# Neighbourhood attention with the weights of its second and last pairs traced ahead, two late query tiles turned in score banks, and two low parts on VectorE

## The chip, the cores and the metric

The kernel runs on one core of a Trainium2 chip. Its time is the device time in microseconds of one execution, and the median of several runs is compared. TensorE multiplies and transposes, VectorE and ScalarE work on what it leaves in its PSUM banks, GpSimd works on SBUF alone, and SyncE (SP) issues most of the transfers between HBM and SBUF.

## What is computed

Two layers of a hybrid backbone act on 1024 latent tokens (a grid of 16 rows and 64 columns) and 128 context tokens, 1152 in all, 1024 features wide, in float32. The first layer has four mLSTM heads and eight grouped-query attention heads, the second sixteen neighbourhood attention heads. Cut to what matters here:

```python
# layer 0, grouped-query part: dense softmax attention of each query block over latent and cached keys
s = einsum('bkgqd,bksd->bkgqs', qi, k) * scale
o = einsum('bkgqs,bksd->bkgqd', softmax(s), v)
# layer 1: each latent token attends to an 8 x 16 window of the grid, with a bias by offset, and to all context keys
q, k, v, z = split(h @ w_in_c, 4)
p = softmax(concat([s_loc + bias, s_ctx]))
o = p_loc @ v_win + p_ctx @ vc
y = (o * silu(z)) @ w_out
# both layers: x = x + gate * rmsnorm(y)
```

## The kernel before, in words

Every projection keeps float32 precision by splitting: an operand is cast to a high part, and the low part is the difference. A product is then three matmuls (high by high, low by high, high by low). `feat` (L367 to L369) gives a projection with features on partitions, 24 matmuls of 128x384 for each of three token chunks; `tok` (L382 to L384, through `rows_by`) gives it with tokens on partitions, 24 matmuls a token tile. `weights` (L121) loads one 512 KB block into one of two `raw` buffers over SP's queue (L126), casts the high part on ScalarE (L115) and subtracts for the low part (L116), on GpSimd unless `vec` is `"lo"`, then on VectorE. The raw buffer is free for the next load when the low part is done.

SBUF tiles of up to 1152 values a partition come from a shared pool of 35 slots (`u`, tag "u"). The three chunks of the normalised input h hold 18 of them in the second layer until the last projection is done. PSUM has eight banks: two for projections (`pj`), three for scores (`s`), one each for `tr` and `ptr`, in which transposes are turned, and one for outputs (`o`).

The program is written as a trace. A scheduler orders each engine's instructions anew, with what was traced earlier ahead of what was traced later, as operands, slots and banks come free in its own simulation; so what is traced behind can still fill a wait of what is traced ahead. On TensorE the grouped-query attention alone is under a manual schedule: its order is the order of the trace.

**Grouped-query attention** (`gqa`, L962). Nine query tiles for each of two groups are projected and turned in `gqa_q`; `turned` (L871) transposes a tile in two halves into bank `tr` or `ptr`, by the tile's parity, casts its high part on ScalarE (L878) and subtracts on VectorE (L879). Tiles 7 and 8 of the second group are kept back in a list and turned in the first iteration of `gqa`. An iteration takes two query tiles: it computes the scores of the next two (L915), turns the probabilities of its own two in ten steps of up to four transposes each (`gqa_turn`, over the banks `tr`, `pj`, `ptr`, `pj` in a cycle, evacuated by ScalarE at L946, each fifth by VectorE at L944), and multiplies them by the values (`gqa_apply`, L955). In the third and fourth head block each iteration also takes one step of `ahead` (L1417), which loads, casts and splits the eight blocks of the first layer's `w_out`.

**First output projection** ("out0", L1422). `load_y` brings a token tile of the mixer's output through a `raw` buffer (L1064), casts it on ScalarE and subtracts on VectorE; `out_half` multiplies it by `w_out` (L382 to L384, operands `yh`, `yl`). One raw buffer holds the gate row (`load_gg`, L1103) for most of that phase.

**Neighbourhood attention** ("na", L1456). The heads go in eight pairs. `na_proj` (L1112) projects a pair's values, queries and keys and `na_pair` (L1224) attends: for each of eight column blocks `na_unit` computes scores of two heads (L1267), adds the bias (VectorE, L1273), takes the exponential (ScalarE, L1275) and its scale (VectorE, L1276; GpSimd, L1277), turns it in `tr` and `ptr` (L107) and multiplies by the values (L1290); a context unit follows (L1031, L1050). The biases of a pair, one for each head, are loaded at the start of `na_pair` (L1230). Pairs 1, 3 and 5 project the values of two pairs at once with `tok` from two blocks of `w_v` (L1184), pair 7 its own with `feat`. A pair's weights are traced inside its own `na_proj`, behind the attention of the pair before; W(0) is the query block, W(1) the keys', W(2) the values', W(3) the gate's.

Of the kernel before, what the change touches and what calls it, by code (L numbers as in the profile page):

```python
# [19 lines left out]
D = 1024  # L20
# [19 lines left out]
class Kern:  # L40
# [378 lines left out]
    def gates(self, gT):  # L419
# [40 lines left out]
        nc.vector.tensor_tensor_scan(b, cst, lf, 0.0, ALU.mult, ALU.add)  # L460
        A, WK, F, M, W = (q5[:, j, :] for j in range(5))
        nc.vector.tensor_tensor(A, li, b, ALU.subtract)
# [43 lines left out]
        nc.vector.tensor_scalar(mi[:72, 1:2], M[:, P - 1 : P], -1.0, None, ALU.mult)  # L506
        nc.scalar.activation(W, M, AF.Exp, bias=mi[:72, 0:1], scale=-1.0)
        nc.scalar.activation(WK, A, AF.Exp, bias=mi[:72, 1:2])
# [342 lines left out]
    def gqa_q(self, h, g, w, Qs, early):  # L851

        nc = self.nc
        ahead = None
        rhs = lambda k: tuple(x[:, (k % 4) * 256 : (k % 4 + 1) * 256] for x in w[k // 4])
        Q = []
        for i in range(NT):
            if i == NT - 4:
                ahead = self.gqa_weights(2) if g == 0 else self.gqa_gate(0)
            if i in (1, 3, 5) and g:  # L860
                n = len(early)
                q0 = Qs[0][n // 2][:, n % 2]
                early.append([])
                for _ in self.gqa_scores([q0[:, hh] for hh in range(2)], 0, lambda s: self.u(s, n="pr"), early[-1]):
                    pass
            ps = self.tok(h, i, rhs, 256)
            q = self.norm_rope(ps, 4, 0, i)
            if i % 2 == 0:
                Q.append(self.u([P, 2, 4, P], F32R, n="Q"))

            def turned(i=i, q=q, Qt=Q[-1]):  # L871
                pt = self.ps(("tr", "ptr")[i % 2])[:, :256]
                for j in range(2):
                    self.flipped(pt[:, j * P : (j + 1) * P], q[:, 2 * j : 2 * j + 2].rearrange("p a b -> p (a b)"))
                for hh in range(2):
                    x = pt[hh * DHB : (hh + 1) * DHB].rearrange("p (a b) -> p a b", b=P)
                    hi, lo = (Qt[r * DHB : (r + 1) * DHB, i % 2, hh::2, :] for r in (g, 1 - g))
                    nc.scalar.copy(hi, x)  # L878
                    nc.vector.tensor_tensor(lo, x, hi.bitcast(F32), ALU.subtract)  # L879

            if g and i in (7, 8):
                self.turned.append(turned)
            else:
                turned()
        return Q, ahead
# [76 lines left out]
    def gqa(self, Q, gz, early, between):  # L962

        kv = lambda j: j // 2
        V = lambda t, j: t[..., kv(j) * DHB : (kv(j) + 1) * DHB]
        q = lambda j, i: [Q[kv(j)][i // 2][:, i % 2, 2 * (j % 2) + hh, :] for hh in range(2)]
        place = (lambda s: self.t("pr", 4, s)), (lambda s: self.u(s, n="pr"))
        todo = iter([(j, i) for j in range(4) for i in range(8)])  # L970

        def tiles(out):
            for j, i in itertools.islice(todo, 2):
                if early:
                    out.append(early.pop(0))
                else:
                    prs = []
                    yield from self.gqa_scores(q(j, i), kv(j), place[i % 2], prs)
                    out.append(prs)

        prs, banks = [], ("tr", "pj", "ptr", "pj")
        for _ in tiles(prs):
            pass
        for j in range(4):
            y = self.ytile()
            for i in range(0, 8, 2):
                if i % 4 == 0:
                    po = self.ps("o")
                nxt, pts = [], ([], [])
                steps = tiles(nxt)  # L990
                turns = self.gqa_turn(prs, pts, banks)
                if i == 4:
                    ctx = self.ctx_steps([self.gqa_terms(x, kv(j), [self.KstP[:, b] for b in range(4)]) for x in q(j, 8)], [V(self.VP, j)] * 2, self.pt, banks=("s", "s"))
                next(steps, None)
                next(steps, None)
                for n, _ in enumerate(turns):
                    if (j, i, n) in ((0, 0, 5), (0, 0, 7)):
                        self.turned.pop(0)()
                    if i == 4 and n == 7 or i == 6 and n == 5:
                        next(ctx)  # L1000
                    if (i, n) != (4, 7):
                        next(steps, None)
                for _ in steps:
                    pass
                self.gqa_apply(pts, V(self.V, j), po[:, i % 4 * P : (i % 4 + 2) * P])
                if i == 6:
                    cpo = next(ctx)
                prs = nxt
                if j >= 2:
                    next(between, None)  # L1010
                if i % 4:
                    self.put_y(4 + j, slice((i - 2) * P, (i + 2) * P), po, gz, y)
            self.put_y(4 + j, slice(8 * P, NT * P), cpo, gz, y)
            gz = self.gqa_gate(j + 1) if j < 3 else None
        return y
# [58 lines left out]

    def w_out(self, l, j):

        return self.weights(self.a["w_out"][l, j], ("", "lo")[j % 2] if l else "")

    def out_half(self, y, w, n, o, ss, gg):
        nc = self.nc  # L1080
# [26 lines left out]
    def na_weights(self, p, b, raw=None):  # L1107
        if raw is not None:
            self.nc.sync.dma_start(raw, self.a["w_c"][4 * p + b])
        return self.weights(self.a["w_c"][4 * p + b], raw=raw)  # L1110

    def na_proj(self, h, p, w):  # L1112
        nc, a = self.nc, self.a
        W = lambda b: self.na_weights(p, b)
        two = lambda t: t[2 * p : 2 * p + 2].rearrange("h t d -> t h d")
        v2 = lambda t: t.rearrange("p (h d) -> p h d", d=DHB)

# [6 lines left out]
        if 0 < p < 7 and p % 2 == 0:  # L1124
            self.feat(h, W(3), zev)
        v = self.u([P, NT, P], n="v") if p in (0, 7) or p % 2 else self.v2
# [12 lines left out]
        q = [self.u([P, T], F32R, n="q") for _ in range(2)]  # L1139
# [40 lines left out]
        if p == 7:  # L1180
            self.feat(h, W(2), vev)
        elif p % 2:

            w = [self.weights(a["w_v"][p // 2, :, q * D : (q + 1) * D]) for q in range(2)]  # L1184
            for i in range(NT):
                ps = self.tok(h, i, lambda k: tuple(x[:, (k % 4) * 256 : (k % 4 + 1) * 256] for x in w[k // 4]), 256)
                nc.scalar.copy(v[:, i, :], ps[:, :P])
                nc.vector.tensor_copy(self.v2[:, i, :], ps[:, P:])
        elif p == 0:

            for cs in ((0, 1), (2,)):
                self.feat(h, w[0], zev, cs)
                self.feat(h, w[1], vev, cs)
        nc.sync.dma_start(two(a["out_nv"]), v2(v[:, 8, :]))
        late = []
        if p < 7:
            self.feat(h, W(0), qev)
            w = W(1)
            self.key_stack2(v2(kc), kx)
            self.feat(h, w, kev)  # L1200
            if p % 2:
                wz = W(3)
                late = [lambda c=c: self.feat(h, wz, zev, [c]) for c in range(NC)]
        else:

            wq, wz = W(0), W(3)
            for w, e, cs in ((wq, qev, [0]), (wz, zev, [0, 1]), (wq, qev, [1])):
                self.feat(h, w, e, cs)
            w = W(1)
            self.key_stack2(v2(kc), kx)  # L1210
            self.feat(h, w, kev)

            late = [lambda w=w, e=e, c=c: self.feat(h, w, e, [c]) for w, e, c in [(wq, qev, 2), (wz, zev, 2)]]

        def terms(hh, j, k0, n):

            x = q[hh][:, j * P : (j + 1) * P]

            ks = lambda t: t[:, k0 : k0 + 4].rearrange("p (a b) k -> p b a k", a=2) if k0 in (2, 6) else t[:, k0 : k0 + n]
            return (x, ks(k[hh])), (x, ks(k[2 + hh]))  # L1220
# [419 lines left out]
```

## Time and profile before

| what | value |
|---|---|
| median of 3 runs | 1527.03 us (1527.02 to 1527.52) |
| profiled execution | 1527.66 us, its span 1525.9 us |
| TensorE busy | 1489.1 us, 98% |
| VectorE, ScalarE, GpSimd busy | 54%, 47%, 29% |
| mean granted TensorE clock | 0.999 |

The profile is of one execution. A row of the timeline gives start and length in us, engine, line, operation, what is written and read, and how often; in brackets the engine's idle time before it and what ended that. PEld is TensorE's loading of weights, which runs beside its matmuls. The end of a matmul is modelled. A row of groups gives, behind the bar, the busy time in us, the mean of one instruction in ns, and the engine's idle time before them.

### The profile page before, as it was taken

The numbers are of one execution on the slowest core, as the hardware profiler recorded it, in microseconds if no ns is written. First come the engines' busy times: TensorE is split into PE (matmuls) and PEld (weight loads), VectorE is DVE, ScalarE is ACT, GpSimd is POOL, SyncE is SP. The second block draws the span as 40 slices with busy tenths as digits, with TensorE's granted clock in tenths as the row PEclk, the third lists the DMA queues.
The fourth block names the chain that finished last, engine by engine and source line by source line (L and its number), as shares of the span: only waits on it lengthen the run. The fifth ranks groups of instructions, "written<-read, shape, count | busy, mean of one in ns | idle before, by whom it ended". The sixth has DMA issues, their size and how long they took to land.

```text
span 1525.9 us, 27070 instructions
## 1 busy us (share of the span) xinstructions
PE 1489.1 (98%) x10139; PEld 1370.8 (90%) x10139; DVE 828.0 (54%) x2387; ACT 711.9 (47%) x1767; POOL 449.3 (29%) x644
## 2 busy tenths in 40 slices
PE   7899999999999999999999999999999999999998
PEld 5799999999999888887888989999999999988786
DVE  5833887963457766665565352535344434445532
ACT  4533535263445777786454352534344344345411
POOL 0001202011135655675224141323132222233200
PEclk9999999999999999999999999999999999999999
DMA  9203546332311000122423222131213121125342
GB/s 378 79 15 130 190 147 239 137 122 75 111 48 44 1 32 24 44 67 70 151 98 137 74 62 80 42 98 31 85 38 104 33 82 69 54 90 167 106 131 83
DMA packets 73284, 143.80 MB, mean 94 GB/s; under 512 B 15737, under 2 KB 44609, under 8 KB 73153
## 3 DMA queue, kind: packets, MB, share of 16 engines
q1 hardware_dynamic: 68566, 126.91, 25.0%
q10 hardware_dynamic: 4586, 15.16, 2.7%
q8 instruction: 80, 1.31, 0.3%
q14 instruction: 52, 0.42, 0.1%
HBM read 115.47 MB, written 21.86 MB: 90 GB/s over the span
## 4 chain that ended last, share of the span: by engine, by line
PE 49%; DMA 1%; DVE 1%; ACT 1%; POOL 1%; issue 0%; DVEq 0%; POOLq 0%; ACTq 0%
PE pj L367 7%; PE pj L368 7%; PE pj L369 7%; PE pj L383 6%; PE pj L382 6%; PE pj L384 6%; PE o L1290 4%; PE s L1267 3%; PE ptr L107 2%; PE tr L107 2%; DMA y<-yd 1%; POOL wlo L116 1%; DMA raw<-in_w_out_dram 0%; DVE sb L1273 0%; POOL pr L925 0%
## 5 line engine op out<-in xcount | busy, mean ns | idle before, releaser
L367 PE MATMUL pj<-hh,whi 128*128 128x384 f32 x1168 | 400.2, 343 | 1.8 <-ACT qT L102 1.2
L368 PE MATMUL pj<-hl,whi 128*128 128x384 f32 x1168 | 397.0, 340 | 0.0
L369 PE MATMUL pj<-hh,wlo 128*128 128x384 f32 x1168 | 395.8, 339 | 0.5 <-DVE wlo L116 0.4
L367 PEld LDWEIGHTS pj<-hh,whi 128*128 128x128 f32 x1168 | 219.6, 188 | 5.5 <-ACT qT L102 1.8
L369 PEld LDWEIGHTS pj<-hh,wlo 128*128 128x128 f32 x1168 | 219.4, 188 | 1.9 <-DVE wlo L116 0.9
L368 PEld LDWEIGHTS pj<-hl,whi 128*128 128x128 f32 x1168 | 219.6, 188 | 1.2
L1277 POOL TENSOR_SCALAR sb<-sb,sm 128x512 f32<-128x512 f32 (+1 forms) x128 | 85.1, 671 | 247.7 <-DVE sm L1276 238.7
L116 POOL TENSOR_TENSOR wlo<-raw,whi 128x1024 fp32r<-128x1024 f32 x43 | 103.0, 2400 | 132.8 <-ACT whi L115 113.7
L925 POOL TENSOR_SCALAR pr<-pr,smg 128x384 f32<-128x384 f32 x192 | 110.0, 591 | 73.9 <-PE pj L107 41.0
L382 PE MATMUL pj<-whi,hh 128*128 128x256 f32 x432 | 122.5, 284 | 0.3 <-DVE nr L783 0.3
L383 PE MATMUL pj<-wlo,hh 128*128 128x256 f32 x432 | 122.5, 284 | 0.0
L384 PE MATMUL pj<-whi,hl 128*128 128x256 f32 x432 | 122.2, 283 | 0.0
L382 PE MATMUL pj<-whi,yh 128*128 128x512 f32 x288 | 114.3, 397 | 2.9 <-DVE o L1085 1.5
L916 DVE CUSTOM_DVE_ANT_0 pr<-s,zero 128x384 f32<-128x384 f32 x192 | 103.8, 553 | 24.3 <-PE s L915 20.9
L383 PE MATMUL pj<-wlo,yh 128*128 128x512 f32 x288 | 113.9, 395 | 0.0
L1275 ACT ACTIVATE sb<-sb,sm 128x512 f32<-128x512 f32 (+1 forms) x128 | 88.9, 695 | 52.9 <-DVE sm L1273 49.3
L384 PE MATMUL pj<-whi,yl 128*128 128x512 f32 x288 | 113.3, 394 | 0.0
L915 PE MATMUL s<-Kst,Q 128*128 128x384 f32 x384 | 107.8, 372 | 1.1 <-ACT pt L1035 1.1
L254 DVE CUSTOM_DVE_ANT_0 mj<-wm,cb 128x512 f32<-128x512 f32 x128 | 89.5, 699 | 5.2 <-DMA wm<-in_w_modT_dram 3.0
L115 ACT CAST whi<-raw 128x1024 fp32r<-128x1024 f32 x77 | 79.7, 1046 | 19.5 <-DMA raw<-in_w_v_dram 6.6
L1273 DVE CUSTOM_DVE_ANT_1 sb<-s,bias 128x512 f32<-128x512 f32 (+1 forms) x112 | 72.9, 664 | 24.9 <-PE ptr L107 12.1
L382 PEld LDWEIGHTS pj<-whi,hh 128*128 128x128 f32 x432 | 81.3, 188 | 1.4 <-issue 0.5
(350 smaller groups left out, 2901.3 us busy)
## 6 DMA issues: line engine op xcount, KB each, us to landing
wm<-in_w_modT_dram SPq DMA_DIRECT2D x32, 512.0 KB, 5.2
raw<-in_w_c_dram SPq DMA_DIRECT2D x25, 512.0 KB, 3.5
raw<-in_w_ab_dram SPq DMA_DIRECT2D x20, 512.0 KB, 3.5
e<-rbd ACTq DMA_DIRECT2D x12, 768.0 KB, 7.7
bias<-in_na_bias_dram SPq DMA_DIRECT2D x16, 576.0 KB, 4.1
wm<-in_w_mod_dram SPq DMA_DIRECT2D x16, 512.0 KB, 9.8
raw<-in_w_out_dram SPq DMA_DIRECT2D x16, 512.0 KB, 3.6
y<-yd SPq DMA_DIRECT2D x18, 448.0 KB, 3.4
```

The costliest lines, as they stand in the source:

```text
L116: (eng_lo or nc.gpsimd).tensor_tensor(lo, src, hi.bitcast(F32), ALU.subtract)
L254: nc.vector.tensor_tensor_reduce(junk, w[:, b, :], cb[:, r, :], 1.0, 0.0, ALU.mult, ALU.add, mp[:, hf, q // 4, 2 * (q % 4) + b, r : r + 1])
L367: nc.tensor.matmul(ps[:, :CW], a, hh, start=k == 0, stop=False)
L368: nc.tensor.matmul(ps[:, :CW], a, hl, start=False, stop=False)
L369: nc.tensor.matmul(ps[:, :CW], b, hh, start=False, stop=k == KB - 1)
L382: nc.tensor.matmul(ps[:, :width], hh, a, start=k == 0, stop=False)
L383: nc.tensor.matmul(ps[:, :width], hh, b, start=False, stop=False)
L384: nc.tensor.matmul(ps[:, :width], hl, a, start=False, stop=k == KB - 1)
L915: nc.tensor.matmul(s[:, :CW], x, y, start=part == 0, stop=part == 1)
L916: nc.vector.tensor_tensor_reduce(pr[:, c, :], s[:, :CW], zero, -1.0, -NEG, ALU.add, ALU.min, m3[:, c : c + 1])
L925: nc.gpsimd.tensor_scalar(pr[:, c, :], pr[:, c, :], r, 0.5, ALU.mult, ALU.mult)
L1275: nc.scalar.activation(x, x, AF.Exp, bias=nm, scale=-1.0, accum_out=r)
```

## The change

Four edits, of which the first two go together:

- the two kept-back query tiles are turned in a score bank (`s`) and no longer in `tr` and `ptr`, and called behind the eighth and tenth turn of the first iteration instead of the sixth and eighth;
- in the first layer the blocks 6 and 7 of `w_out` get their low part on VectorE; the second layer's blocks alternate as before;
- the two value blocks of pair 1 are traced at the end of pair 0's projections, ahead of pair 0's attention;
- the value, query and gate blocks of pair 7 are traced at the end of pair 6's projections, ahead of pair 6's attention; its key block stays where it was.

```diff
--- before.py
+++ after.py
@@ -869,7 +869,7 @@
                 Q.append(self.u([P, 2, 4, P], F32R, n="Q"))
 
             def turned(i=i, q=q, Qt=Q[-1]):
-                pt = self.ps(("tr", "ptr")[i % 2])[:, :256]
+                pt = self.ps("s" if g and i in (7, 8) else ("tr", "ptr")[i % 2])[:, :256]
                 for j in range(2):
                     self.flipped(pt[:, j * P : (j + 1) * P], q[:, 2 * j : 2 * j + 2].rearrange("p a b -> p (a b)"))
                 for hh in range(2):
@@ -994,7 +994,7 @@
                 next(steps, None)
                 next(steps, None)
                 for n, _ in enumerate(turns):
-                    if (j, i, n) in ((0, 0, 5), (0, 0, 7)):
+                    if (j, i, n) in ((0, 0, 7), (0, 0, 9)):
                         self.turned.pop(0)()
                     if i == 4 and n == 7 or i == 6 and n == 5:
                         next(ctx)
@@ -1074,7 +1074,7 @@
 
     def w_out(self, l, j):
 
-        return self.weights(self.a["w_out"][l, j], ("", "lo")[j % 2] if l else "")
+        return self.weights(self.a["w_out"][l, j], "lo" if (j % 2 if l else j >= 6) else "")
 
     def out_half(self, y, w, n, o, ss, gg):
         nc = self.nc
@@ -1109,9 +1109,12 @@
             self.nc.sync.dma_start(raw, self.a["w_c"][4 * p + b])
         return self.weights(self.a["w_c"][4 * p + b], raw=raw)
 
+    def v_weights(self, p):
+        return [self.weights(self.a["w_v"][p // 2, :, q * D : (q + 1) * D]) for q in range(2)]
+
     def na_proj(self, h, p, w):
         nc, a = self.nc, self.a
-        W = lambda b: self.na_weights(p, b)
+        W = lambda b: self.w7[b] if p == 7 and b in self.w7 else self.na_weights(p, b)
         two = lambda t: t[2 * p : 2 * p + 2].rearrange("h t d -> t h d")
         v2 = lambda t: t.rearrange("p (h d) -> p h d", d=DHB)
 
@@ -1181,7 +1184,7 @@
             self.feat(h, W(2), vev)
         elif p % 2:
 
-            w = [self.weights(a["w_v"][p // 2, :, q * D : (q + 1) * D]) for q in range(2)]
+            w = self.wv if p == 1 else self.v_weights(p)
             for i in range(NT):
                 ps = self.tok(h, i, lambda k: tuple(x[:, (k % 4) * 256 : (k % 4 + 1) * 256] for x in w[k // 4]), 256)
                 nc.scalar.copy(v[:, i, :], ps[:, :P])
@@ -1211,6 +1214,11 @@
             self.feat(h, w, kev)
 
             late = [lambda w=w, e=e, c=c: self.feat(h, w, e, [c]) for w, e, c in [(wq, qev, 2), (wz, zev, 2)]]
+
+        if p == 0:
+            self.wv = self.v_weights(1)
+        if p == 6:
+            self.w7 = {b: self.na_weights(7, b) for b in (2, 0, 3)}
 
         def terms(hh, j, k0, n):
```

## Rows read from the trace of the kernel before

**Rows 1.** The page, part 1: busy us (share of the span) and instructions.

```profile
PE 1489.1 (98%) x10139; PEld 1370.8 (90%) x10139; DVE 828.0 (54%) x2387; ACT 711.9 (47%) x1767; POOL 449.3 (29%) x644
```

**Rows 2.** Sums by window; header names the columns, (x) counts instructions.

```profile
core 0: us, PE busy (x) PEld busy (x) DVE busy (x) ACT busy (x) POOL busy (x), PEclk, DMA share, GB/s
512.70:523.60 10.90, 7.42 (x55) 6.01 (x54) 7.54 (x30) 10.46 (x27) 9.13 (x16) 1.00 0.00 0
702.20:714.60 12.40, 12.40 (x113) 9.26 (x114) 6.04 (x14) 8.44 (x17) 8.65 (x9) 1.00 0.39 121
714.60:716.30 1.70, 0.37 (x7) 0.13 (x3) 0.91 (x3) 0.94 (x1) 0.00 (x0) 1.00 0.05 13
859.90:877.30 17.40, 17.40 (x102) 17.40 (x101) 6.19 (x13) 5.50 (x12) 1.50 (x2) 1.00 0.26 86
877.30:888.00 10.70, 8.09 (x43) 5.44 (x41) 9.36 (x30) 8.50 (x20) 5.61 (x7) 1.00 0.15 34
888.00:919.60 31.60, 31.60 (x323) 30.40 (x323) 12.11 (x40) 13.15 (x35) 12.50 (x14) 1.00 0.20 64
1337.10:1355.60 18.50, 16.79 (x189) 14.28 (x188) 11.13 (x35) 11.33 (x27) 7.05 (x10) 1.00 0.06 22
```

**Rows 3.** Timeline, TensorE, first iteration of grouped-query attention.

```profile
519.71 0.41 PE L107 MATMUL ptr<-cc,nr 128*128 128x128 f32 x2 [0.95 <-ACT pt L946]
519.95 0.60 PE L107 MATMUL pj<-cc,pr 128*128 128x128 f32 x4
520.39 0.60 PE L107 MATMUL tr<-cc,pr 128*128 128x128 f32 x4
522.44 0.41 PE L107 MATMUL tr<-cc,nr 128*128 128x128 f32 x2 [1.45 <-ACT pt L946]
...
523.57 4.11 PE L955 MATMUL o<-pt,V 128*64 128x256 f32 x36
```

**Rows 4.** Timeline, ScalarE, the same stretch.

```profile
519.43 1.29 ACT L922 ACTIVATE pr<-pr,smg 128x1152 f32<-128x1152 f32 x1
...
523.32 0.59 ACT L946 COPY pt<-pj 128x512 f32<-128x512 f32 x1
```

**Rows 5.** Timeline, four engines, up to the first output projection.

```profile
705.37 1.06 ACT L115 CAST whi<-raw 128x1024 fp32r<-128x1024 f32 x1
...
709.45 2.37 POOL L116 TENSOR_TENSOR wlo<-raw,whi 128x1024 fp32r<-128x1024 f32 x1
...
711.85 11.51 SPq L1064 DMA_DIRECT2D y<-yd  x3
...
715.31 0.94 ACT L115 CAST yh<-y 128x896 fp32r<-128x896 f32 x1 [4.08 <-DMA y<-yd]
...
716.30 0.50 PE L382 MATMUL pj<-whi,yh 128*128 128x512 f32 x1 [1.33 <-ACT yh L115]
```

**Rows 6.** Groups by line and shape, whole span.

```profile
L367 PE MATMUL pj<-hh,whi 128*128 128x384 f32 x1168 | 400.2, 343 | 1.8 <-ACT qT L102 1.2 <-DVE kl L1170 0.3 <-DVE vT L104 0.2
...
L116 DVE TENSOR_TENSOR wlo<-raw,whi 128x1024 fp32r<-128x1024 f32 x34 | 42.6, 1254 | 12.9 <-ACT whi L115 9.6 <-DMA wm<-in_w_mod_dram 2.3 <-PE pj L368 0.8
```

**Rows 7.** Timeline, four engines, attention of pair 0.

```profile
880.36 0.47 PE L1267 MATMUL s<-k,q 128*128 128x512 f32 x1 [0.99 <-DVE sm L1276]
...
887.98 0.48 PE L1267 MATMUL s<-k,q 128*128 128x512 f32 x1 [0.97 <-issue]
...
860.84 0.33 SPq L126 DMA_DIRECT2D raw<-in_w_v_dram  x1
...
887.03 1.03 ACT L115 CAST whi<-raw 128x1024 fp32r<-128x1024 f32 x1
...
889.16 2.40 POOL L116 TENSOR_TENSOR wlo<-raw,whi 128x1024 fp32r<-128x1024 f32 x1
```

**Rows 8.** Timeline, two engines, attention of pair 6.

```profile
1303.15 0.33 SPq L126 DMA_DIRECT2D raw<-in_w_c_dram  x1
...
1352.77 1.99 ACT L115 CAST whi<-raw 128x1024 fp32r<-128x1024 f32 x2
```

## The prediction

> **What bounds the kernel.** I read the page's busy line first: TensorE is busy 98% of the span and no other engine over 54% [rows 1]. So only time in which TensorE starts no matmul can be won, and I looked for that stretch by stretch: the list of TensorE's waits gives their names, the sums by window their size, the timeline what ends each. Before 512 us the diff changes nothing. After it the windows show four stretches with TensorE idle [rows 2]: 512.7 to 523.6 (7.42 us busy of 10.90), 714.6 to 716.3 (0.37 of 1.70), 877.3 to 888.0 (8.09 of 10.70) and 1337.1 to 1355.6 (16.79 of 18.50). The stretch right behind the third, 888.0 to 919.6, is the same kind of work and full. In each of the four the diff changes something; I call them A, B, C and D.
>
> A visible gap is shorter than the loss, since a matmul's modelled end runs past the start of the next: four transposes stand with 0.60 us, yet the next four start 0.44 us after them [rows 3]. So I add 0.16 us to each gap.
>
> **A, the two late query tiles.** Tiles 7 and 8 of the second query group are turned by two transposes each, placed by hand between the ten turns of the first iteration. Tile 7's wait 0.95 us and tile 8's 1.45 us [rows 3]; both wait for ScalarE's copy out of the very bank that they are to write, which a turn filled just before. ScalarE is the late one: busy 10.46 of the stretch's 10.90 us [rows 2], with an exponential of 1.29 us ahead of the copies [rows 4]. The change gives both a score bank (no more scores are due in this iteration, so these banks are empty) and calls them two turns later. Removed: 0.95 + 1.45 + 2 x 0.16 = 2.7 us. Added: nothing; transposes, casts and subtractions are as many as before. What is late next: the value matmuls (L955) behind the turns need ScalarE's last copy, which ended at 523.91, and they started at 523.57 [rows 3, 4]. ScalarE may keep that time, with the tiles' short casts ahead of the copy. But in their 4.11 us the value matmuls come to that copy only after some two thirds, 2.7 us, so they can begin near 521.2 even then: 2.4 us won. The score banks must be empty when the next scores come, behind the value matmuls, and ScalarE and VectorE have those 4.11 us for it. Bounds: 0 (if the copies slip with the casts) and 2.7; I take 2.7, since the copies' rows lie close.
>
> **B, two low parts on VectorE.** At the first output projection TensorE idles 1.33 us until ScalarE has cast y, which waited 4.08 us for y's load; that load was issued at 711.85, when GpSimd's subtraction for the last w_out block (709.45, 2.37 us) had freed the raw buffer [rows 5]. On VectorE the same subtraction takes 1.25 us [rows 6], and its input, the cast of 705.37, is there at 706.43. VectorE is busy 6.04 of 12.40 us there [rows 2], so two subtractions, 2.5 us, fit; even if the second waits 1.25 us for other work it ends by 709.0, and the load starts 2.8 us earlier. Load and cast take 716.30 - 711.85 = 4.45 us and TensorE could start at 714.8 (the gap taken off), so 710.3 is early enough. Removed 1.33 + 0.16 = 1.5 us. GpSimd is relieved of 2 x 2.37 us where it feeds the last turns. Bounds 0 (the load is late for another reason) and 1.5; I take 1.5.
>
> **C, value weights of pair 1 ahead.** In 877.3 to 888.0 pair 0's attention runs almost alone: 2.61 us idle in five gaps, the first at 880.36, the last at 887.98, between score matmuls that wait for the softmax chain on the other engines [rows 2, 7]. What covers attention later, pair 1's value projection, needs both weight halves. The second half's raw load was issued at 860.84, yet its cast ran at 887.03 and its low part ended at 891.56 [rows 7]; it is traced behind attention. Traced ahead, the cast can follow the load, near 865 to 870, and two casts and two low parts (2 x 1.03 and 2 x 2.40 us) leave the softmax chain too. Where they go, 859.9 to 877.3, ScalarE is busy 5.50 and GpSimd 1.50 of 17.40 us [rows 2], under the key projection, which TensorE computes without a gap. On SP's queue pair 0's biases may come behind the raw load of 860.84; a load of about this size lands in 3.5 us (711.85 to 715.31, [rows 5]), so 869 at the latest, ahead of the scores. Shared slots: 18 for h, 4 for pair 0's gate, values and queries, 4 for its two weights, 4 new ones, 2 biases: 32 of 35. Removed: 2.61 + 5 x 0.16 = 3.4 us. Bounds 0 and 3.4; I take 3.4, because the next stretch, where the same filler is at hand, has no gap at all. The filler lasts: behind 919.6 the value projection still goes on alone, so using 3.4 us of it early uncovers nothing.
>
> **D, weights of pair 7 ahead.** The same in pair 6's attention: its filler, pair 7's value projection, is spent at 1337.1. Behind it 1.71 us are idle in four gaps, while the raw loads of the next weights, the last issued at 1303.15, wait for casts at 1352.77 [rows 2, 8]. Cast ahead they give 72 matmuls of 0.34 us less 0.16 [rows 6], 13 us of filler, for gaps of 1.71 + 4 x 0.16 = 2.35 us. One gap of the four stands among transposes of the value tiles, which weights don't touch; I take three quarters, 1.8 us, with bounds 0 and 2.35. GpSimd gets up to three low parts (7.2 us) ahead of pair 6's scalings, again under the key projection.
>
> **Sum.** 2.7 + 1.5 + 3.4 + 1.8 = 9.4 us. The profiled execution took 1527.66 us (span 1525.9), so 1518.3; the median of the runs is 0.63 us lower: **1517.6 us**. TensorE's granted clock is 1.00 in every window, the upper of its two levels (2.4 GHz).
>
> **Rivals.**
> First: the scheduler keeps the casts behind the exponentials, or lays the fillers elsewhere. For it: raw loads stood issued for 26 us in C and 49 us in D before their casts [rows 7, 8], so something other than the load decides. Then A and B alone: 2.7 + 1.5 = 4.2, 1522.8 us; with half of C and D 1520.2.
>
> Second, slower: the slots run out. Pair 6's six new weight tiles are traced ahead of its two biases: 18 for h, 4 for the score rings, 4 for the pair, 4 for its own weights and these 6 are 36 of 35. The biases then wait for the key projection's weights, the fillers are spent while attention waits, and it runs uncovered at the pace of 877.3 to 888.0, 3.4 us lost in 10.70. Over as long an attention as pair 0's, 877.3 to 919.6, that is 13.4 us, 11.0 more than D's 2.35 now. With A, B and C won (7.6) it comes to 1530.5. It decides as soon as the biases land after the fillers end. Against: SP may still issue the biases first, since they wait for nothing but slots, and pair 0 has room for all.
>
> Third: as much is lost in new places, since the last pair has gaps behind VectorE and ScalarE that any reordering moves. Then 1524 to 1530, no change.
>
> Fourth: more is won. In the four stretches weight loads are busy far less than matmuls: 10.90 - 6.01, 1.70 - 0.13, 10.70 - 5.44 and 18.50 - 14.28, 15.9 us free together, of which a covered stretch would keep 3.8% (31.60 - 30.40) [rows 2]. If all that were won, 14.4 us: 1512.6. Against: between the gaps matmuls already follow at full pace. The Trainium skill (Perfetto Trace Analysis, Identifying the Most-Contended Engine) speaks for it: matmul busy share is called a poor measure of headroom there, the busy share of weight loads a good one; by it the sum is 14.4 where mine is 9.4.
>
> **How the numbers follow.** My forecast, all four stretches mostly won, 60%: 1515.5 to 1520. First rival 19%, 1520 to 1524. Fourth 7%. Third 9%. Second 5%. A measurement here can tell about 0.2%, 3.05 us, from no change; so faster is the forecast, the first and the fourth: 86%, same 9%, slower 5%. The range goes from a little under the forecast's own to most of the first rival: 1514.5 to 1523.5.
>
> **What would show it.** A: the transposes of tiles 7 and 8 without idle time before them, L955 starting near 521 instead of 523.57. B: the y load issued before 710 and no gap before L382. C: both casts of the value weights before 877, and L382 to L384 between pair 0's score matmuls from the first one on. D: the casts of pair 7 before 1320, and L367 to L369 between 1337 and 1352. Wrong would be: biases landing after the key projection, TensorE waiting for a low part, or gaps of the same sum elsewhere.

## The result and the profile after

The changed kernel takes 1517.74 us (median of 6 runs, 1515.79 to 1520.05), the kernel before 1527.16 us beside it (6 runs, 1526.24 to 1529.14); the ratio is 0.9937 with an interval of 0.9924 to 0.9950. The forecast was 1517.6 us. The profiled execution took 1517.94 us, its span 1516.2.

The page, part 1, of the changed kernel, against [rows 1]:

```profile
PE 1486.5 (98%) x10139; PEld 1371.4 (90%) x10139; DVE 827.4 (55%) x2389; ACT 712.6 (47%) x1767; POOL 447.1 (29%) x642
```

Sums by window of the changed kernel, against [rows 2]; the stretches are moved to where the same work now stands (A, the start of B, C, D and the end of D):

```profile
core 0: us, PE busy (x) PEld busy (x) DVE busy (x) ACT busy (x) POOL busy (x), PEclk, DMA share, GB/s
511.30:519.40 8.10, 7.04 (x54) 6.03 (x52) 6.30 (x27) 7.98 (x22) 7.43 (x13) 1.00 0.01 2
709.50:711.90 2.40, 2.40 (x18) 1.39 (x17) 0.82 (x4) 0.00 (x0) 0.00 (x0) 1.00 0.36 99
872.00:882.60 10.60, 10.60 (x79) 9.94 (x79) 6.57 (x24) 5.95 (x15) 3.42 (x6) 1.00 0.14 32
...
1328.60:1347.00 18.40, 18.40 (x155) 17.44 (x155) 8.34 (x27) 8.33 (x19) 4.47 (x7) 1.00 0.03 12
1347.00:1356.00 9.00, 8.21 (x99) 7.25 (x95) 5.28 (x13) 4.92 (x11) 1.98 (x3) 1.00 0.26 89
```

B, C and D are full now; in A 1.06 us stay idle (two waits that stood before the turns and that nothing touches), and 0.79 us at the end of D: 0.44 us ahead of transposes of probabilities and 0.35 us ahead of transposes of values, both behind ScalarE's copy at L102.

Idle time alone does not say what a part is worth. Every trace here has 10139 TensorE matmul records, so the record with the same number (counted from 0) marks the same amount of work done; each stretch of the table also holds the same matmuls before and after, but for the bank of the two query tiles. The table gives the time from start to start of such records, in us (the first column from the start of the span), for the two kernels and all experiments; the letters are the parts of the change that fall into a stretch:

```
record      0-3250   -3500  -4750  -5000   -5500   -6250   -8750   -9500  -10138
                       A              B               C               D
before        504.55  36.08 162.27  45.92  100.23  105.31  333.67  109.96  121.25
before_again  504.47  36.07 162.27  46.15  100.24  106.31  333.67  110.02  121.41
after         503.18  33.29 162.27  45.19  100.33  101.57  334.02  108.17  121.52
after_again   503.59  33.30 162.28  45.63  100.33  101.57  334.02  107.93  120.68
a_only        503.14  33.31 162.29  45.99  100.34  105.53  333.63  110.33  120.74
a_bank        505.87  33.64 162.27  45.92  100.23  105.35  333.67  110.30  121.19
a_late        504.50  38.51 162.29  46.00  100.33  105.48  333.63  110.15  120.61
b_only        503.27  36.07 162.27  45.76  100.30  106.37  333.92  110.39  120.71
c_only        505.62  36.07 162.27  46.03  100.23  101.60  333.97  110.10  121.03
d_only        503.52  36.07 162.27  46.02  100.24  105.34  333.67  108.36  121.14
d_all         504.00  36.09 162.27  45.94  100.23  106.32  333.67  110.42  120.92
y_pool        502.90  33.30 162.28  45.00  100.32  101.57  334.02  108.28  121.28
plus          503.80  33.30 162.27  45.00  100.32  101.57  334.02  108.09  121.40
plus_bank     504.61  33.62 162.26  44.96  100.29  101.68  333.92  108.15  121.18
```

Between before and after the parts win 2.79 (A), 0.73 (B), 3.74 (C) and 1.79 us (D), 9.05 together. Another 1.37 us is won ahead of record 3250, where the change touches nothing, and 0.72 us is given back in the stretches between the parts and at the end: 9.70 in all.

The timeline of the changed kernel shows how. TensorE and ScalarE in A, against [rows 3, 4]:

```profile
518.25 0.38 PE L107 MATMUL s<-cc,nr 128*128 128x128 f32 x2
518.47 0.60 PE L107 MATMUL pj<-cc,pr 128*128 128x128 f32 x4
518.91 0.38 PE L107 MATMUL ptr<-cc,pr 128*128 128x128 f32 x2
519.12 0.38 PE L107 MATMUL s<-cc,nr 128*128 128x128 f32 x2
519.44 0.87 PE L955 MATMUL o<-pt,V 128*64 128x256 f32 x6
...
520.43 0.36 ACT L878 CAST Q<-s 64x256 fp32r<-64x256 f32 x1
520.82 0.59 ACT L946 COPY pt<-pj 128x512 f32<-128x512 f32 x1
```

Both tiles are turned without a wait (the `s` rows). Their casts (L878) run under the value matmuls (L955), the first of them ahead of the last turn's copy (L946). The value matmuls start right behind the last transpose, as they did before (523.57 in [rows 3] has no idle time before it either).

C and D, against [rows 7, 8]: casts of the weights, one filler of each, and pair 6's biases (L1238 is L1230 of the kernel before, L1275 its L1267). A filler is a matmul of the next pair's projections that is laid between matmuls of attention.

```profile
852.51 2.00 ACT L115 CAST whi<-raw 128x1024 fp32r<-128x1024 f32 x2
...
859.62 1.05 ACT L115 CAST whi<-raw 128x1024 fp32r<-128x1024 f32 x1 [2.07 <-DMA raw<-in_w_v_dram]
...
873.16 0.28 PE L382 MATMUL pj<-whi,hh 128*128 128x256 f32 x1
...
1297.25 1.05 ACT L115 CAST whi<-raw 128x1024 fp32r<-128x1024 f32 x1 [1.42 <-DMA raw<-in_w_c_dram]
...
1298.76 0.38 SPq L1238 DMA_DIRECT2D bias<-in_na_bias_dram  x1
...
1309.53 0.33 SPq L1238 DMA_DIRECT2D bias<-in_na_bias_dram  x1
...
1338.22 0.34 PE L368 MATMUL pj<-hl,whi 128*128 128x384 f32 x1
```

The last cast of pair 1's value weights starts at 859.62 in place of 887.03, and L382 follows pair 0's first scores at 873.16. The last cast of the three blocks of pair 7 starts at 1297.25 in place of 1352.77, and L367 to L369 go on filling pair 6's attention from 1338.22.

### The profile page after: what moved, and what is told of

The parts are those of the page before. It is cut to its first block, busy times and chain, and to the rows that moved or that the text cites. A ratio compares the mean times of both kernels' runs of the same rounds, so it can differ in the third digit from the quotient of the medians.

```text
span 1516.2 us, 27083 instructions
## 1 busy us (share of the span) xinstructions
PE 1486.5 (98%) x10139; PEld 1371.4 (90%) x10139; DVE 827.4 (55%) x2389; ACT 712.6 (47%) x1767; POOL 447.1 (29%) x642
## 4 chain that ended last, share of the span: by engine, by line
PE 51%; DMA 1%; ACT 1%; DVE 1%; POOL 0%; issue 0%; DVEq 0%; POOLq 0%
PE pj L367 7%; PE pj L368 7%; PE pj L369 7%; PE pj L383 6%; PE pj L382 6%; PE pj L384 6%; PE o L1298 4%; PE s L1275 3%; PE ptr L107 2%; PE tr L107 2%; DMA y<-yd 1%; PE o L955 1%; DMA raw<-in_w_out_dram 1%; POOL wlo L116 0%; ACT whi L115 0%
## 5 line engine op out<-in xcount | busy, mean ns | idle before, releaser
L367 PE MATMUL pj<-hh,whi 128*128 128x384 f32 x1168 | 400.3, 343 | 1.9 <-ACT qT L102 1.2
L369 PE MATMUL pj<-hh,wlo 128*128 128x384 f32 x1168 | 395.6, 339 | 0.4 <-DVE wlo L116 0.4
L367 PEld LDWEIGHTS pj<-hh,whi 128*128 128x128 f32 x1168 | 219.5, 188 | 5.6 <-ACT qT L102 1.8
L369 PEld LDWEIGHTS pj<-hh,wlo 128*128 128x128 f32 x1168 | 219.3, 188 | 1.8 <-DVE wlo L116 0.6
L116 POOL TENSOR_TENSOR wlo<-raw,whi 128x1024 fp32r<-128x1024 f32 x41 | 98.3, 2403 | 127.9 <-ACT whi L115 92.4
L925 POOL TENSOR_SCALAR pr<-pr,smg 128x384 f32<-128x384 f32 x192 | 112.1, 601 | 71.2 <-PE pj L107 38.1
L382 PE MATMUL pj<-whi,hh 128*128 128x256 f32 x432 | 123.0, 285 | 0.3 <-DVE nr L783 0.3
L382 PE MATMUL pj<-whi,yh 128*128 128x512 f32 x288 | 114.3, 397 | 1.5 <-DVE o L1085 1.5
L382 PEld LDWEIGHTS pj<-whi,hh 128*128 128x128 f32 x432 | 81.4, 188 | 1.5 <-issue 0.6
```

Of the source, the lines that this page charges most:

```text
L116: (eng_lo or nc.gpsimd).tensor_tensor(lo, src, hi.bitcast(F32), ALU.subtract)
L367: nc.tensor.matmul(ps[:, :CW], a, hh, start=k == 0, stop=False)
L369: nc.tensor.matmul(ps[:, :CW], b, hh, start=False, stop=k == KB - 1)
L382: nc.tensor.matmul(ps[:, :width], hh, a, start=k == 0, stop=False)
L925: nc.gpsimd.tensor_scalar(pr[:, c, :], pr[:, c, :], r, 0.5, ALU.mult, ALU.mult)
```

## The experiments

### Each part alone

The lines of each diff that matter; the helper functions are as in the change.

```diff
# a_only
+                pt = self.ps("s" if g and i in (7, 8) else ("tr", "ptr")[i % 2])[:, :256]
+                    if (j, i, n) in ((0, 0, 7), (0, 0, 9)):
# b_only
+        return self.weights(self.a["w_out"][l, j], "lo" if (j % 2 if l else j >= 6) else "")
# c_only
+        if p == 0:
+            self.wv = self.v_weights(1)
# d_only
+        if p == 6:
+            self.w7 = {b: self.na_weights(7, b) for b in (2, 0, 3)}
```

> Only the two late query tiles are changed (score banks, two turns later). Theory (each edit works in its own stretch and the parts add up): from the first score matmul of grouped-query attention to its first value matmul (L955) 2.7 us less than before, and nothing else: about 1524.4 us. Rival 1 (ScalarE gives the time back behind the turns, since it stays the late engine): under 1 us less there, about 1526.5. Rival 2 (the 1.41 us that the changed kernel gained at 268 us, at a wait for ScalarE's hs in the mLSTM part, which no edit touches, belongs to the change): it shows here too, or in one of the other three, and the total is 1.4 lower; by the theory it belongs to the execution and falls to any kernel or none.

> Only the low parts of blocks 6 and 7 of w_out are moved to VectorE. Theory after reading the changed kernel: the 1.6 us from the last L1050 to the first L382 of the output projection go, but 0.3 to 0.5 us are given back where two of its matmuls are laid between value matmuls (0.34 us from start to start in place of 0.23) and 0.24 us at a later wait for VectorE's L1085; 0.6 to 0.8 us less by the end of the output projection, total about 1526.3. Rival (the forecast's term): 1.5 us less, and the smaller gain in the changed kernel came from the other parts shifting it.

> Only the two value blocks of pair 1 are traced ahead. Theory (filler): L382 to L384 stand between pair 0's score matmuls from the first ones on, no idle TensorE from 872 to 900, 3.4 to 3.7 us less by the middle of the value projection, total about 1523.5. Rival (what is pulled forward is missed later, as the same matmuls fill the waits at the end of pair 0's attention): the gain shrinks behind 910 us to under 2 us, total above 1525.

> Only the value, query and gate blocks of pair 7 are traced ahead. Theory: the score wait near 1345 goes and pair 7's L367 to L369 stand in pair 6's attention; 1.5 to 1.8 us less by the output projection, total about 1525.4; the two idle stretches of 0.6 us among the value transposes near 1351 stay. Rival 1 (the slots run out and pair 6's biases are late): 5 to 11 us more. Rival 2 (the gain there needs the other parts, by another order of the queues): under 0.5 us.

The medians of 11 runs each, against 1527.33 us before (33 runs): A 1525.59 (ratio 0.9988, 0.9979 to 0.9997), B 1526.39 (0.9995, 0.9986 to 1.0003), C 1523.58 (0.9976, 0.9967 to 0.9985), D 1525.52 (0.9992, 0.9983 to 1.0001). They give 1.74, 0.94, 3.75 and 1.81 us, 8.2 together; A's median lies 1.2 us above the 1524.4 expected, and the intervals of B and D include no change. Single runs of one kernel lie up to 5 us apart, so the table decides the sizes. There A wins 2.77, C 3.71 and D 1.60 us, near what they win in the changed kernel: each acts in its own stretch and they add up. B alone wins 0.16 us, less than the 0.6 to 0.8 expected. Rival 2 of the first run falls: the stretch ahead of 3250 is shorter in A, B and D alike, and longer in C, though their work there is the same.

What B gives back shows in b_only's timeline:

```profile
723.48 0.94 ACT L115 CAST yh<-y 128x896 fp32r<-128x896 f32 x1 [6.47 <-DMA y<-yd]
...
724.33 0.59 ACT L1084 ACTIVATE x<-pj 128x512 f32<-128x512 f32 x1
...
724.46 1.09 DVE L116 TENSOR_TENSOR yl<-y,yh 128x896 fp32r<-128x896 f32 x1 [5.86 <-ACT yh L115]
...
725.47 0.68 DVE L1085 TENSOR_TENSOR x<-pj,raw 128x512 f32<-128x512 f32 x1
...
726.20 0.50 PE L382 MATMUL pj<-whi,yh 128*128 128x512 f32 x1 [0.53 <-DVE x L1085]
```

The cast and the subtraction of the third y tile, whose load is late, now stand ahead of the first L1084 and L1085, which empty a projection bank. Both engines wait 6 us for a transfer with work behind them, and TensorE then waits for the bank: 0.92 us from start to start of its matmuls in place of the usual 0.23. In the changed kernel the same wait costs 0.24 us.

### The third y tile off the two engines: y_pool

```diff
# on the changed kernel, for y tile 2 of the first output projection alone
-        self.split(hi[:, :n], lo[:, :n], y[:, :n], eng_lo=nc.vector)
+            nc.gpsimd.tensor_copy(hi[:, :n], y[:, :n])
+            nc.gpsimd.tensor_tensor(lo[:, :n], y[:, :n], hi[:, :n].bitcast(F32), ALU.subtract)
```

> The changed kernel, with the third y tile of the output projection cast and subtracted on GpSimd (idle there) in place of ScalarE and VectorE. Theory (half of part B's gain is lost because that tile's cast and subtraction stand ahead of the first L1084 and L1085 on ScalarE and VectorE and wait for its load): the wait of TensorE for VectorE's L1085 (0.24 us in the changed kernel, 0.89 us with part B alone) goes, and the stretch from the last score matmul of grouped-query attention to the middle of the output projection is 0.2 to 0.3 us shorter than in the changed kernel; total about 1517.5. Rival (the wait is ScalarE's or VectorE's own load of work): it stays.

The timeline of y_pool:

```profile
717.00 0.60 ACT L1088 ACTIVATE x<-pj 128x512 f32<-128x512 f32 x1 [3.15 <-PE pj L384]
...
717.72 0.69 DVE L1089 TENSOR_TENSOR x<-pj,raw 128x512 f32<-128x512 f32 x1 [2.28 <-ACT x L1088]
...
719.91 0.93 POOL L1068 CAST yh<-y 128x896 fp32r<-128x896 f32 x1 [15.12 <-DMA y<-yd]
```

The bank is emptied as soon as it is full, at 717.7 (L1089 is L1085 there), before the third tile has landed. The stretch is 45.00 us against 45.19, the lower end of the 0.2 to 0.3 us expected, and the same in plus (45.00) and plus_bank (44.96). So a part of what B lacks is shown: the order on ScalarE and VectorE. Without that wait B is worth 0.92 us, with it 0.73 or, alone, 0.16. The time, 1517.51 us (0.9933, 0.9917 to 0.9950), cannot be told from the changed kernel's.

### Bank or place: a_bank and a_late

```diff
# a_bank: the bank alone
-                pt = self.ps(("tr", "ptr")[i % 2])[:, :256]
+                pt = self.ps("s" if g and i in (7, 8) else ("tr", "ptr")[i % 2])[:, :256]
# a_late: the place alone
-                    if (j, i, n) in ((0, 0, 5), (0, 0, 7)):
+                    if (j, i, n) in ((0, 0, 7), (0, 0, 9)):
```

> Of part A the bank alone: tiles 7 and 8 are turned in score banks, but called at the old places (behind the sixth and eighth turn). Theory (the wait was for the bank that a turn had just filled): the waits of 0.95 and 1.45 us go and the first value matmul comes at least 2.2 us earlier against the first score matmul (61.10 us in the kernel before, 58.38 in the changed one); total about 1524.7. Rival (it takes both, since ScalarE's casts at the old places put off the copies behind them): the turns after the tiles wait for ScalarE instead, under 1.5 us won.

> Of part A the place alone: the tiles are called behind the eighth and tenth turn, still in the transpose banks. Theory (bank): each stands again behind a turn that has just filled its bank, so the two waits stay in size; 0 to 0.7 us won, total 1526.5 to 1527.5. Rival (the place is what counts): 2 us or more won from the first score matmul to the first value matmul.

By the table the bank alone wins 2.44 us of A's 2.77, the place 0.33 on top of it; the median with the bank alone is 1525.52 us against 1527.47 (10 and 25 runs; 0.9989, 0.9979 to 0.9998). The place alone loses 2.43 us: 1529.17 us (10 runs; 1.0014, 1.0004 to 1.0023). There 0 to 0.7 us won was expected, so that expectation was missed. TensorE's timeline and the windows of a_late:

```profile
519.64 0.41 PE L107 MATMUL ptr<-cc,nr 128*128 128x128 f32 x2
519.89 0.60 PE L107 MATMUL pj<-cc,pr 128*128 128x128 f32 x4
523.71 0.41 PE L107 MATMUL ptr<-cc,pr 128*128 128x128 f32 x2 [3.21 <-DVE Q L879]
```

```profile
519.00:524.00 5.00, 1.78 (x16) 1.38 (x14) 1.12 (x5) 4.03 (x9) 2.93 (x6) 1.00 0.00 0
...
525.00:528.40 3.40, 3.40 (x20) 1.93 (x18) 0.61 (x2) 0.37 (x1) 0.00 (x0) 0.51 0.02 5
```

At the later place a tile in `ptr` stands in front of the last turn, which needs that bank, and it is freed only by two casts and two subtractions: one wait of 3.21 us in place of two of 0.95 and 1.45 [rows 3]. The first value matmul comes 0.79 us later against the first score matmul (61.89 against 61.10 us). The rest, 1.6 us, is lost behind it, where the granted clock falls to 0.51 for 3.4 us, the lower of its two levels (1.2 GHz).

### How short the slots are: d_all

```diff
-            self.w7 = {b: self.na_weights(7, b) for b in (2, 0, 3)}
+            self.w7 = {b: self.na_weights(7, b) for b in (2, 0, 3, 1)}
```

> Part D with pair 7's key block as a fourth one traced ahead: 8 weight tiles ahead of pair 6's two biases, 38 of 35 slots by the forecast's count. With three blocks the biases were already issued late (the second at 1316.89 against 1291.77 in the kernel before) and cost nothing, since they landed ahead of the end of the fillers near 1330. Theory (the price starts only when the biases land behind the fillers): the second bias comes later still, by one freed pair of weight tiles; if it lands before 1330 the time is as with three blocks, about 1525.4, if behind it the attention of pair 6 runs uncovered. Rival (second rival of the forecast): 5 to 11 us slower than before, 1532 to 1538.

The issue of the second bias on SP, and two windows of d_all:

```profile
1333.15 0.34 SPq L1233 DMA_DIRECT2D bias<-in_na_bias_dram  x1
```

```profile
1314.00:1340.00 26.00, 25.94 (x149) 25.57 (x149) 7.01 (x21) 6.12 (x15) 4.78 (x6) 1.00 0.31 91
1348.00:1358.00 10.00, 9.14 (x98) 7.66 (x96) 7.60 (x26) 6.96 (x19) 5.30 (x8) 1.00 0.06 21
```

The second bias is issued 16 us later than with three blocks alone (1316.89 in d_only), and the fillers are spent before attention gets going: TensorE is full to 1340 and waits behind it. D's stretch is 110.42 us, 2.06 more than in d_only and 0.46 more than before: the fourth block takes back all that the three won. The median is 1528.23 us (1.0002, 0.9993 to 1.0011), no gain. The mechanism is that of the forecast's second rival; its price is 2 us and not the 5 to 11 that were expected of it.

### The same kernels again: before_again, after_again

Both unchanged, one execution each.

> The kernel before, unchanged, in another profiled execution. Theory (the 1.4 us at 268 us and the stretches at half the granted clock are the execution's own): same order, the same four waiting stretches with the same lengths within 0.1 us (61.1 us from the first score matmul to the first value matmul), but the wait near 268 us may be gone, then everything behind it 1.4 us earlier, or a stretch of 3.41 us at clock 0.50 may stand somewhere in or behind a wait of TensorE. Rival (the wait at 268 us belongs to the kernel before): it is there again with 0.79 us.

> The changed kernel, unchanged, in another profiled execution. Theory: part by part the same gains as in its first profile within 0.1 us (58.4 us from the first score matmul to the first value matmul, 3.5 us in pair 0, 1.5 to 1.8 us in pair 6), whatever stands ahead of 460 us. Rival (the gains of the parts are themselves chance of one execution): one of them differs by over 0.5 us.

A, C and D come out within 0.25 us of the first profiles, where 0.1 was expected, but for C in before_again, 1.0 us longer at a fallen clock. B comes out within 0.5 (0.29 us won against the first before): it hangs on when the y loads land (ScalarE waited 6.51 us for the third tile's in after_again, 5.90 in after), so its size in one profile is partly chance. The wait near 268 us is gone in before_again, so it is the execution's own: 1529.02 us all the same, because its clock fell twice. Windows of before_again:

```profile
53.40:56.80 3.40, 3.28 (x11) 3.09 (x12) 3.40 (x8) 2.10 (x5) 0.00 (x0) 0.50 0.01 2
882.80:886.20 3.40, 3.40 (x15) 2.91 (x13) 2.62 (x10) 3.16 (x8) 2.20 (x5) 0.50 0.13 27
```

### Further in the same manner: plus and plus_bank

```diff
# plus: y_pool, and in pair 7's value projection
-            pt = self.ps("ptr")
+            pt = self.ps("s" if p == 7 and c else "ptr")
# plus_bank: plus with the tiles called at the old places
```

> The changed kernel with the third y tile split on GpSimd and, after the manner of part A, the last two chunks of pair 7's values turned in score banks (their transposes wait 0.35 us for ScalarE's copy out of the bank, behind a wait of 0.44 us of the probabilities). Theory (bank waits): the wait of 0.35 us goes, 0.2 to 0.5 us less behind pair 6 than with the third y tile alone; total 1517.0, which the runs can't tell from 1517.5. Rival (pair 7's first scores then wait for their banks, or the copies are the bound): nothing or a loss there.

> The same, with the two late query tiles called at their old places (score banks alone). With part A alone the bank gave 2.9 us up to the first value matmul and 2.4 us up to matmul 3500, both edits gave 2.8. Theory (the place adds little): 0 to 0.4 us longer than the version with both, from the first score matmul to matmul 3500; total within 0.5 us of it. Rival (the place costs, as it does without the bank): 0.2 us or more shorter.

plus: 1518.00 us (0.9933, 0.9921 to 0.9944), plus_bank 1518.42 (0.9936, 0.9925 to 0.9948); neither can be told from the changed kernel. The aim of plus was missed. Timeline of plus:

```profile
1351.03 0.49 PE L107 MATMUL s<-cc,vT 128*128 128x128 f32 x3
...
1352.72 0.55 PE L107 MATMUL ptr<-cc,vT 128*128 128x128 f32 x3 [0.35 <-ACT pt L102]
```

The 0.35 us are still there: the transposes that wait are those of the first chunk, which kept its bank (`ptr`). The other two chunks, now in `s`, stand without idle time in the changed kernel too (1353.90 and 1359.01), so there was nothing to win in them. D's stretch is 0.19 us shorter than in y_pool, within what two executions differ by. plus_bank repeats a_bank: 33.62 against 33.30 us, 0.3 us for the place. No version beats the changed kernel by more than the runs can tell.

## Why the prediction was right

**The total** lies 0.1 us from the forecast, but not each step does, and so close a hit is in part luck: B fell 0.8 us short, A, C and D came out 0.4 us over together, and single runs lie up to 5 us apart. The parts give 9.05 us of the 9.4 forecast. That the profiles differ by 9.7 is 1.37 us of chance ahead of the change, less 0.72 given back between the parts.

**A, right:** 2.79 us against 2.7. "Both wait for ScalarE's copy out of the very bank that they are to write" is what a_bank shows. ScalarE, busy 7.98 of 8.10 us, took only one of the tiles' casts ahead of its last copy, and that under the value matmuls, so the bound of 0 did not come. What the step left out is the place as a cost of its own: with a free bank it gives 0.33 us, with the old ones it costs 2.4.

**B, wrong by half:** the term of 1.5 us measured 0.73, 0.29 and, alone, 0.16. The wait for ScalarE's first cast went as forecast, with the load issued at 703.55. The term was mis-sized at "Removed 1.33 + 0.16 = 1.5 us", with nothing set against it: the step looked at whether "two subtractions, 2.5 us, fit" on VectorE and not at what the earlier loads would do to the order behind it. The timeline of the changed kernel, at L1085 and at the first matmuls:

```profile
703.55 0.38 SPq L1064 DMA_DIRECT2D y<-yd  x1
...
707.68 0.94 ACT L115 CAST yh<-y 128x896 fp32r<-128x896 f32 x1 [1.22 <-DMA y<-yd]
...
709.53 0.51 PE L382 MATMUL pj<-whi,yh 128*128 128x512 f32 x1
...
709.88 0.40 PE L383 MATMUL pj<-wlo,yh 128*128 128x512 f32 x1
...
720.05 0.94 ACT L115 CAST yh<-y 128x896 fp32r<-128x896 f32 x1 [5.90 <-DMA y<-yd]
...
722.77 0.19 PEld L382 LDWEIGHTS pj<-whi,yh 128*128 128x128 f32 x1 [0.40 <-DVE x L1085]
```

The third y tile's cast at 720.05 puts off L1084, and TensorE waits for L1085 at 722.77 (the 0.40 us in the row is idle time of the weight loads; its matmuls lose 0.24); y_pool takes that away and has 0.92 us. Most of the other 0.58 us goes where two matmuls are laid among the value matmuls (709.53 and 709.88: 0.35 us from start to start, where the ones behind follow at 0.23). From start to start, the four L1050 ahead of the old wait take 1.19 us less in the stretch than before and the transposes into `tr` 0.12 less, but the 65 value matmuls take 0.37 us more and the 135 of the projection 0.22 more: 0.7 us in all. So a second thing was left out of the term: the matmuls that start early do so in the middle of other work.

**C, right:** 3.74 us in its stretch, 3.71 alone, against 3.4. "Using 3.4 us of it early uncovers nothing" held: by record 8750, 0.35 us is given back, but b_only, which has no part C, gives back 0.25 there as well.

**D, right in mechanism, its size partly luck:** 1.79, 2.03 and, alone, 1.60 us against 1.8. The four gaps of the kernel before:

```profile
1345.57 0.33 PE L1031 MATMUL s<-k,q 128*128 128x128 f32 x1 [0.63 <-DVE sm L1273]
1347.65 0.44 PE L1290 MATMUL o<-pt,v 128*64 128x128 f32 x4 [0.28 <-ACT pt L102]
1351.84 0.52 PE L107 MATMUL ptr<-cc,sb 128*128 128x128 f32 x3 [0.44 <-ACT pt L102]
1352.93 0.55 PE L107 MATMUL ptr<-cc,vT 128*128 128x128 f32 x3 [0.35 <-ACT pt L102]
```

The step let one gap of the four stay; the last two stayed, with the same 0.44 and 0.35 us. By the step's own sum the first two are worth 0.63 + 0.28 + 2 x 0.16 = 1.2 us. Most of the rest came from where no gap stood: the same 428 matmuls of L367 to L369 take 0.47 us less from start to start.

**The rivals.** The first (casts stay late) fell: they ran 27 and 55 us earlier, of which 5 and 8 us are what all work there had gained. The second came half true. The biases went out 8 and 18 us later than before, where the forecast's reason against it was that SP may issue them first. Their issue before:

```profile
1290.57 1.59 SPq L1230 DMA_DIRECT2D bias<-in_na_bias_dram  x2
```

SP's wait for the second in the changed kernel (us in total, times, longest), from the list of SP's waits between 1285 and 1330:

```profile
SPq L1238 <- PE pj L369: 2.1, 1, 2.1
```

The second waited for the key projection's last L369, as it would for a slot that a weight tile holds, and was issued at 1309.53 as that projection ended. So one of the forecast's signs of being wrong, "biases landing after the key projection", did come. The first stood on SP right behind the raw load of pair 7's key block (1298.34), so SP's order alone may have put it off. It cost nothing, most likely because fillers were left when they landed; one block more is enough to lose D's gain (there the second bias waited 7.7 us for an L369). The price of 11 us was too high: attention ran uncovered for a part of its length, for 2 us. The third had 0.72 us in it, no more. The fourth fell: the parts gave 9.05 us of its 14.4, though 1.85 us idle stay in the stretches. The rule of the Trainium skill beside it (Perfetto Trace Analysis, Identifying the Most-Contended Engine) pointed at the right stretches, but the sum of waits from start to start gave their size.

## What to carry to other kernels

Trace ahead what can fill a wait, and count the slots to the last tile: three blocks paid and the fourth took all back. When a transfer is freed early, look at which in-order queues now hold its cast ahead of the work that empties a bank. A short step that borrows a bank from a busy rotation needs a bank of its own more than a better place.

## What the runs showed of the hardware

**Waits of TensorE cost more than their length, by chance.** The stretch behind the uncovered part of pair 0's attention ran at half clock in three traces of the eight without part C (before_again, b_only, d_all) and in none of the six with it; each time the stretch was 1.0 us longer. Windows of b_only:

```profile
876.50:881.30 4.80, 3.25 (x15) 1.93 (x15) 4.49 (x15) 2.82 (x7) 1.28 (x2) 1.00 0.23 55
881.30:884.70 3.40, 3.40 (x14) 2.91 (x13) 2.59 (x8) 3.15 (x7) 2.27 (x4) 0.51 0.09 22
```

0.51 is the lower of the clock's two levels (1.2 GHz). The kernel before has much the same waits there (8.09 us busy of 10.70 in [rows 2]), and its clock stayed at 1.00. So C is worth 1 us more in some executions than its stretch shows, and a_late's single wait of 3.21 us was followed by a loss of 1.6 us beyond itself. The Trainium skill (TensorE: Matmul & The Clock Gate, HAM oscillation) says that waits between bursts send the clock back to its lower level; these rows agree for three of the eight traces with the waits, and five show no fall.

**Two profiles differ where the program doesn't.** The stretch to record 3250 lies between 502.90 and 505.87 us. Four of the fourteen traces have the wait for ScalarE's hs near 268 us, worth 1.4 to 2.0 us, and four a fall of the clock near 53 us, worth 1.5, as before_again has. A saving of under 1 us is read by stretch, not by the total.

**A short VectorE instruction waited out GpSimd's.** The timeline of before, then the same cast and the next of its kind in the changed kernel:

```profile
705.41 2.38 POOL L116 TENSOR_TENSOR wlo<-raw,whi 128x1024 fp32r<-128x1024 f32 x1
...
705.61 2.27 DVE L113 CAST yh<-y 128x128 fp32r<-128x128 f32 x1
```

```profile
703.44 0.61 DVE L113 CAST yh<-y 128x128 fp32r<-128x128 f32 x1
...
709.66 0.22 DVE L113 CAST yh<-y 128x128 fp32r<-128x128 f32 x1
```

The cast takes 0.22 us where GpSimd does nothing beside it. Before, it took 2.27 us and ended 0.09 us behind GpSimd's subtraction; in the changed kernel the subtraction is on VectorE, and it took 0.61 us and ended 0.08 us behind a shorter GpSimd scaling (L925, 702.36 to 703.98). The Trainium skill (SBUF — State Buffer, Terms) says that the two engines share a port pair that one holds for a whole instruction; the rows agree. That would speak for moving such a subtraction even where GpSimd has time; no run here shows what it is worth.
